# A two-layer decoder trunk on one core: scores and values on parts of the array, first loads by single chunks, bias loads on another queue

## The chip, the cores and the metric

The kernel runs on one core of one Trainium2 chip. The metric is the device time of one execution in microseconds, as the median of several runs. The core has five engines that work side by side and meet at semaphores: TensorE (PE, matmuls; PEld is its load of the stationary operand), VectorE (DVE), ScalarE (ACT), GpSimd (POOL) and SyncE (SP, which here only issues DMAs). Each takes its instructions in the order in which they are written.

## The reference, cut to what matters

The input is 256 tokens of 1024 float32 numbers. Two layers follow, each an attention and a squared-ReLU MLP, with a layer norm behind each:

```python
h = x
for layer in range(2):
    if layer == 0:
        mix = diff_attention(h, ...)       # 8 heads, two maps each, difference of two softmaxes
    else:
        kv = shared_kv(h, w_kv_shared)     # 16 heads of 64
        mix = moba_attention(h, ...)       # here: causal softmax over the one block of 256 keys
    h = layer_norm(ALPHA * h + mix, ...)
    h = layer_norm(ALPHA * h + square(relu(h @ w_up)) @ w_down, ...)
```

All logits get a bias that depends on the distance of query and key (one table for both layers), and the causal mask. In both layers there are 16 maps with a head dimension of 64; the kernel takes them in 8 pairs.

## The kernel before

Weights come as 96 units of 1 MiB, each in two pieces of 128x1024 float32 (`raw`), five of which are in flight or waiting. Each number is split in two: ACT copies the piece to float32r (`whi`, L101), DVE takes the difference (`wlo`, L113). Up to seven split units lie ready. A product is three matmuls that accumulate in PSUM, hi\*hi, hi\*lo, lo\*hi (`three`, L135; lines 139 to 141 and 143 to 145). Every load of a piece is issued on SP's queue (`fetch`, L88) as soon as the piece five earlier has been split; until then that queue stands still, and what is behind it too.

The order on every engine is the order of the program text. `attention` (L334) begins with the V projection. In layer 0 its first two units are taken as they arrive (`v_first`, L377): x comes transposed in four loads of 128x512, each with two loads of 128x512 of a unit. Per step of two chunks, ACT and DVE split x and weights, and TensorE does four hi\*hi matmuls (L395), then the rest (L401, L402). Four matmuls on zeros (L180) run ahead of them. After the first step a product of the bias table with a one-hot matrix, 33 rows by 16 columns (`make_lines`, L187), gives one line per head. DVE copies them out (L188), and ACT's queue copies them 32 times to DRAM, four heads first, twelve later (`copy_lines`, L191), so that tiles with one diagonal per row can be loaded from there (`load_bias`, L198: four loads of 64 KB per pair, on SP's queue, two tiles in turn).

Then a loop over i = 0 to 7 runs a pipeline on pairs: `project(i)` makes Q and K of pair i, transposed, Q's two heads on partitions 0 to 63 and 64 to 127, K's likewise. `halves_hi(i-1)` and `halves_lo(i-1)` split them, `softmax_a(i-2)` adds the bias and takes the exponentials, `softmax_b(i-2)` scales, `turn` and `turned` transpose the maps, `scores(i-1)` and `values(i-3)` end the iteration. For one pair both heads' scores are made at once: the keys lie in `kz`, 128 rows by two halves of 256 columns, where head m's keys fill rows 64m to 64m+63 of half m and zeros fill the rest (memsets on GpSimd, L351). So `halves` needs two ACT copies (L458) and two DVE differences (L468) of 64 rows:

```python
nc.tensor.matmul(s, qh[:, q], kh[:, :, :n], start=True, stop=False)    # L478
nc.tensor.matmul(s, qh[:, q], kl[:, :, :n], start=False, stop=False)   # L479
nc.tensor.matmul(s, ql[:, q], kh[:, :, :n], start=False, stop=True)    # L480
```

once with n = 256 for the later 128 queries (512 columns) and once with n = 128 for the earlier ones (256 columns). Layer 1's values lie in `V` with zeros between the two heads of a pair (L345), and `values` makes both heads' transposed values in one PSUM region with float32 matmuls of 128 stationary columns (L561 to L564). `make_lambda` (L212) loads the four lambda vectors on GpSimd's queue, `rms` runs a reciprocal root on GpSimd (L265 on), `ln_params` (L298) loads the norms' parameters there.

Of the kernel before, what the change touches and what calls it, by code (L numbers as in the profile page):

```python
# [53 lines left out]
def trunk(ctx: ExitStack, tc: tile.TileContext, x, xT, units, lam_a, subln, rel_bias,  # L54
# [13 lines left out]
    def split_to(hi, lo, src, scale=None):  # L68
        """hi + lo = scale * src, both float32r."""
# [13 lines left out]
    def fetch(q):  # L83
        """Piece q's load."""
# [5 lines left out]
    def head():  # L90
        """The hi half of the next piece."""
# [13 lines left out]
    def piece():  # L105
        """The lo half of the next piece, after the hi half of a later one."""
# [12 lines left out]
    def bg(most=8, force=False):  # L119
        """Pieces of later units, as many as the products since the last ones have room for."""  # L120
# [45 lines left out]
    for q in range(4):  # L166
        raws[q] = wpool.tile([P, PIECE], F32, name="raw", bufs=RAWS)
        c = slice(q * 512, (q + 1) * 512)
        nc.sync.dma_start(xTr[:, c], xT[:, c])
        for j in range(2):  # L170
            d = (q % 2) * PIECE + j * 512
            nc.sync.dma_start(raws[q][:, j * 512:(j + 1) * 512], units[q // 2][:, d:d + 512])
# [822 lines left out]
```

## Time and profile before

| | |
|---|---|
| Median of 3 runs | 622.54 us (620.99 to 622.95) |
| Span of the profiled execution, first to last instruction | 621.2 us |
| TensorE busy | 603.8 us, 97% |
| DVE, ACT, GpSimd busy | 385.8, 325.5, 15.4 us |
| DMA | 113.86 MB, mean 183 GB/s |

The profiled execution's time is its span; what lies around it is 1.3 us, if the median of the runs is taken for its time. Starts in the views are microseconds from the span's start. A matmul's duration holds its way through the array, so the pitch from one start to the next says what it costs; weight loads run beside matmuls. A number in brackets at a row's end is the time that the engine sat idle ahead of it, with what ended that.

### The profile page before, as it was taken

Reading aid. Unit: us, or ns where it says so; the run is one execution under the profiler, and the core shown is the slowest. Engines: PE = TensorE matmul, PEld = TensorE weight load, DVE = VectorE, ACT = ScalarE, POOL = GpSimd, SP = SyncE. Lnnn points to the kernel's source line nnn. Section 1 sums busy time; section 2 is a strip of 40 time slices with the busy share of each in tenths; the row PEclk is TensorE's granted clock in tenths of the full one; section 3 lists DMA queues with packets and bytes.
Section 4 is the critical chain, followed back from the end, with each engine's and each line's share of the span. In section 5 each row is a group of like instructions: output and inputs, shape, how many; then the busy total and the mean of one; then the engine's idle time right before and its main releaser. Section 6 shows DMA issues by size and latency. Waiting matters only on the chain.

```text
span 621.2 us, 9556 instructions
## 1 busy us (share of the span) xinstructions
PE 603.8 (97%) x3674; PEld 533.2 (86%) x3674; DVE 385.8 (62%) x706; ACT 325.5 (52%) x556; POOL 15.4 (2%) x40
## 2 busy tenths in 40 slices
PE   8999999999999999999999999999999999999994
PEld 5998987888898899898889899988898898899883
DVE  5479888877634734653877577877767534544236
ACT  5477787447654754552346466462586654554200
POOL 2000011000000000000020000000000000000000
PEclk9999999999999999999999999999999999999998
DMA  8797684547666556556258655341588656553001
GB/s 298 226 312 233 199 257 153 187 169 238 200 222 221 177 197 238 194 178 204 68 165 286 205 157 170 103 143 60 166 303 267 216 179 207 177 181 103 1 0 69
DMA packets 36985, 113.86 MB, mean 183 GB/s; under 512 B 4603, under 2 KB 9756, under 8 KB 36940
## 3 DMA queue, kind: packets, MB, share of 16 engines
q1 hardware_dynamic: 35056, 108.02, 52.9%
q0 software_dynamic: 1264, 4.39, 2.1%
q10 hardware_dynamic: 620, 0.84, 0.4%
q8 instruction: 29, 0.48, 0.3%
q14 instruction: 16, 0.13, 0.1%
HBM read 111.40 MB, written 1.84 MB: 182 GB/s over the span
## 4 chain that ended last, share of the span: by engine, by line
PE 74%; issue 10%; DMA 7%; DVE 5%; ACT 2%; POOL 1%; SPq 0%; DVEq 0%; POOLq 0%; ACTq 0%
PE ps_a L140 11%; PE ps_a L139 11%; PE ps_a L141 11%; PE ps_b L143 9%; PE ps_b L145 9%; PE ps_b L144 9%; DMA raw<-in_units 5%; PE ps_b L141 3%; PE ps_b L139 3%; PE ps_b L140 3%; DVE wlo L113 2%; DMA bias<-scr 1%; ACT whi L101 1%; PE ps_c L288 1%; PE ps_c L533 1%
## 5 line engine op out<-in xcount | busy, mean ns | idle before, releaser
L113 DVE TENSOR_TENSOR wlo<-raw,whi 128x1024 fp32r<-128x1024 f32 x188 | 222.8, 1221 | 66.6 <-ACT whi L101 66.1
L101 ACT ACTIVATE whi<-raw 128x1024 fp32r<-128x1024 f32 x188 | 190.4, 1053 | 83.8 <-PE ps_a L141 49.7
L143 PE MATMUL ps_b<-act_hi,whi 128*128 128x256 f32 x640 | 182.4, 285 | 0.0
L145 PE MATMUL ps_b<-act_hi,wlo 128*128 128x256 f32 x640 | 180.2, 282 | 0.0
L144 PE MATMUL ps_b<-act_lo,whi 128*128 128x256 f32 x640 | 179.9, 281 | 0.0
L144 PEld LDWEIGHTS ps_b<-act_lo,whi 128*128 128x128 f32 x640 | 120.6, 188 | 0.6
L143 PEld LDWEIGHTS ps_b<-act_hi,whi 128*128 128x128 f32 x640 | 120.5, 188 | 0.6
L145 PEld LDWEIGHTS ps_b<-act_hi,wlo 128*128 128x128 f32 x640 | 120.5, 188 | 0.0
L139 PE MATMUL ps_a<-whi,h_hi 128*128 128x512 f32 x248 | 98.5, 397 | 0.0
L141 PE MATMUL ps_a<-whi,h_lo 128*128 128x512 f32 x248 | 98.3, 396 | 0.0
L140 PE MATMUL ps_a<-wlo,h_hi 128*128 128x512 f32 x248 | 98.3, 396 | 0.0
L72 DVE TENSOR_TENSOR h_lo<-sqr,h_hi 128x512 fp32r<-128x512 f32 x24 | 16.6, 692 | 80.5 <-ACT h_hi L70 80.5
L141 PEld LDWEIGHTS ps_a<-whi,h_lo 128*128 128x128 f32 x248 | 46.7, 188 | 11.3
L140 PEld LDWEIGHTS ps_a<-wlo,h_hi 128*128 128x128 f32 x248 | 46.8, 189 | 10.8
L139 PEld LDWEIGHTS ps_a<-whi,h_hi 128*128 128x128 f32 x248 | 46.7, 188 | 10.8
L762 ACT ACTIVATE relu<-ps_b 128x512 f32<-128x512 f32 x32 | 19.1, 596 | 67.1 <-PE ps_b L145 56.8
L500 ACT ACTIVATE t<-t,mx 128x256 f32<-128x256 f32 x64 | 28.4, 444 | 34.5 <-DVE mx L497 34.5
L139 PE MATMUL ps_b<-whi,act_hi 128*128 128x512 f32 x96 | 39.4, 410 | 0.4 <-ACT act_hi L70 0.4
L141 PE MATMUL ps_b<-whi,act_lo 128*128 128x512 f32 x96 | 38.0, 396 | 1.0 <-DVE act_lo L74 1.0
L140 PE MATMUL ps_b<-wlo,act_hi 128*128 128x512 f32 x96 | 37.9, 395 | 0.0
L139 PE MATMUL ps_a<-whi,act_hi 128*128 128x512 f32 x80 | 32.5, 407 | 0.0
L140 PE MATMUL ps_a<-wlo,act_hi 128*128 128x512 f32 x80 | 31.6, 395 | 0.0
(142 smaller groups left out, 628.4 us busy)
## 6 DMA issues: line engine op xcount, KB each, us to landing
raw<-in_units SPq DMA_DIRECT2D x188, 512.0 KB, 5.2
bias<-scr SPq DMA_DIRECT2D x64, 64.0 KB, 4.2
raw<-in_units SPq DMA_DIRECT2D x8, 256.0 KB, 5.3
lnp<-in_ln_g POOLq DMA_DIRECT2D x4, 512.0 KB, 4.3
lnp<-in_ln_b POOLq DMA_DIRECT2D x4, 512.0 KB, 4.9
xres<-in_xT SPq DMA_DIRECT2D x4, 256.0 KB, 5.2
xres<-in_x SPq DMA_DIRECT2D x1, 1024.0 KB
scr<-lnp ACTq DMA_DIRECT2D x1, 576.0 KB
```

Of the source, the lines that this page charges most:

```text
L72: nc.vector.tensor_tensor(lo, src, hi.bitcast(F32), op=ALU.subtract)
L101: nc.scalar.activation(split[v][0][:, c], raws[state["head"]], AF.Copy)
L113: nc.vector.tensor_tensor(split[v][1][:, c], raws.pop(state["piece"]), split[v][0][:, c].bitcast(F32), op=ALU.subtract)
L139: nc.tensor.matmul(ps, a[0], w[0], start=start, stop=False)
L140: nc.tensor.matmul(ps, a[0], w[1], start=False, stop=False)
L141: nc.tensor.matmul(ps, a[1], w[0], start=False, stop=stop)
L143: nc.tensor.matmul(ps, w[0], a[0], start=start, stop=False)
L144: nc.tensor.matmul(ps, w[0], a[1], start=False, stop=False)
L145: nc.tensor.matmul(ps, w[1], a[0], start=False, stop=stop)
L288: nc.tensor.transpose(pt[:, j * P:(j + 1) * P], src[:, j * P:(j + 1) * P], ident)
L500: nc.scalar.activation(t[:, m, s], t[:, m, s], AF.Exp, bias=mx[:, m, j:j + 1], accum_out=sm[:, m, j:j + 1])
L762: nc.scalar.activation(r, ps, AF.Relu)
```

## The change

Four things are changed; everything else is as it was, apart from line numbers and comments.

- The first loads: x comes in eight loads of one chunk (128x256), each with one 128x512 block of a unit. `v_first` works chunk by chunk: split x and weights, two hi\*hi, two lo\*hi, two hi\*lo. Behind the hi\*hi of the first two chunks stands one more matmul on zeros. The bias lines are made after the fifth chunk, copied out of PSUM after both units.
- `copy_lines` and `load_bias` are issued on GpSimd's queue.
- `scores` takes keys without zeros (`kh`, `kl`, 128x256): each head's matmul has the 64 rows in which it lies, the two heads go in turn into two PSUM banks. K is split ahead of Q, in one instruction on ACT and one on DVE.
- In layer 1, `V` has no zeros, and `values` writes each head's 64 PSUM rows with 64 stationary columns.

```diff
-    for q in range(4):
-        raws[q] = wpool.tile([P, PIECE], F32, name="raw", bufs=RAWS)
-        c = slice(q * 512, (q + 1) * 512)
-        nc.sync.dma_start(xTr[:, c], xT[:, c])
-        for j in range(2):
-            d = (q % 2) * PIECE + j * 512
-            nc.sync.dma_start(raws[q][:, j * 512:(j + 1) * 512], units[q // 2][:, d:d + 512])
+    for k in range(NK):
+        if k % 2 == 0:
+            raws[k // 2] = wpool.tile([P, PIECE], F32, name="raw", bufs=RAWS)
+        nc.sync.dma_start(xTr[:, k * S:(k + 1) * S], xT[:, k * S:(k + 1) * S])
+        nc.sync.dma_start(raws[k // 2][:, (k % 2) * 512:(k % 2 + 1) * 512],
+                          units[k // 4][:, (k % 4) * 512:(k % 4 + 1) * 512])
...
     def make_lines():
         nc.tensor.matmul(pb[:NH, :RELS], table, oh[:NBUCKET + 1], start=True, stop=True)
-        nc.vector.tensor_copy(line, pb[:NH, :RELS])
...
-        nc.scalar.dma_start(scr[:, h0:h1].rearrange("p h r -> h p r"),
+        nc.gpsimd.dma_start(scr[:, h0:h1].rearrange("p h r -> h p r"),
...
-            nc.sync.dma_start(b[g:g + COPIES],
+            nc.gpsimd.dma_start(b[g:g + COPIES],
...
+                    a = [at(kk, h) for h in range(2)]
+                    for h in range(2):
+                        nc.tensor.matmul(pv[0, h], a[h][0], hi[:, k], start=kk == 0, stop=False)
+                    if kk < 2:
+                        nc.tensor.matmul(warm[:, :P], zero[:, :P], zero[:, :P], start=True, stop=True)
+                    for h in range(2):
+                        nc.tensor.matmul(pv[0, h], a[h][1], hi[:, k], start=False, stop=False)
+                    for h in range(2):
+                        nc.tensor.matmul(pv[0, h], a[h][0], lo[:, k], start=False, stop=kk == NK - 1)
+                    if kk == 4:
                         make_lines()
...
                 v_first(0)
+                v_first(1)
+                nc.vector.tensor_copy(line, pb[:NH, :RELS])
                 copy_lines(0, 4)
-                v_first(1)
...
+                k = (pool.tile([P, S], F32R, name="kh"), pool.tile([P, S], F32R, name="kl"))
+                nc.scalar.activation(k[0], ps[:, 1], AF.Copy)
                 nc.scalar.activation(q[0], ps[:, 0], AF.Copy, scale=0.125)
-                for m in range(2):
-                    r = slice(m * 64, (m + 1) * 64)
-                    nc.scalar.activation(kz[p % 2][0][r, m], ps[r, 1], AF.Copy)
...
+                sc = [bank("a") for _ in range(2)]
+                for c, n, t in ((0, 256, 1), (256, 128, 0)):
                     q = tokens(t)
-                    nc.tensor.matmul(s, qh[:, q], kh[:, :, :n], start=True, stop=False)
-                    nc.tensor.matmul(s, qh[:, q], kl[:, :, :n], start=False, stop=False)
-                    nc.tensor.matmul(s, ql[:, q], kh[:, :, :n], start=False, stop=True)
+                    for i, (a, b) in enumerate(((qh, kh), (qh, kl), (ql, kh))):
+                        for m in range(2):
+                            r = slice(m * 64, (m + 1) * 64)
+                            nc.tensor.matmul(sc[m][:, c:c + n], a[r, q], b[r, :n], start=i == 0, stop=i == 2)
...
-                v = [slice((3 * p + m) * 64, (3 * p + m + 2) * 64) for m in range(2)]
-                nc.tensor.matmul(o, V[:, 0, v[0]], a[:, 0, 0:256], start=True, stop=False)
-                nc.tensor.matmul(o[:, 128:], V[:, 1, v[0]], a[:, 0, 256:384], start=False, stop=False)
-                nc.tensor.matmul(o[:, 128:], V[:, 1, v[1]], a[:, 1, 256:384], start=False, stop=False)
-                nc.tensor.matmul(o, V[:, 0, v[1]], a[:, 1, 0:256], start=False, stop=True)
+
+                r = [slice(m * 64, (m + 1) * 64) for m in range(2)]
+                v = [slice((2 * p + m) * 64, (2 * p + m + 1) * 64) for m in range(2)]
+                for m in range(2):
+                    nc.tensor.matmul(o[r[m]], V[:, 0, v[m]], a[:, m, 0:256], start=True, stop=False)
+                for m in range(2):
+                    nc.tensor.matmul(o[r[m], 128:], V[:, 1, v[m]], a[:, m, 256:384], start=False, stop=True)
```

On TensorE, in layer 1, the scores of one pair and the values of another stand side by side. Before (shapes are rows of the result by columns; `kz` has a tile's number behind it):

```order
L145 MATMUL ps_b<-act_hi,wlo 128x256
L478 MATMUL ps_a<-kz_3156,qh 128x512 [waits PE_49,Activation_49]
L479 MATMUL ps_a<-kz_3157,qh 128x512 [waits DVE_49]
L480 MATMUL ps_a<-kz_3156,ql 128x512
L478 MATMUL ps_a<-kz_3156,qh 128x256 [waits PE_49]
L479 MATMUL ps_a<-kz_3157,qh 128x256
L480 MATMUL ps_a<-kz_3156,ql 128x256
L561 MATMUL ps_a<-aT,V 128x256 [waits Activation_49]
L562 MATMUL ps_a<-aT,V 128x128
L563 MATMUL ps_a<-aT,V 128x128 [waits DVE_49]
L564 MATMUL ps_a<-aT,V 128x256
L143 MATMUL ps_b<-act_hi,whi 128x256
```

The same place now:

```order
L145 MATMUL ps_b<-act_hi,wlo 128x256
L455 MATMUL ps_a<-kh,qh 128x256 [waits Activation_49]
L455 MATMUL ps_a<-kh,qh 128x256
L455 MATMUL ps_a<-kl,qh 128x256 [waits DVE_49]
L455 MATMUL ps_a<-kl,qh 128x256
L455 MATMUL ps_a<-kh,ql 128x256 [waits DVE_49]
L455 MATMUL ps_a<-kh,ql 128x256
L455 MATMUL ps_a<-kh,qh 128x128 x2
L455 MATMUL ps_a<-kl,qh 128x128 x2
L455 MATMUL ps_a<-kh,ql 128x128 x2
L539 MATMUL ps_a<-aT,V 64x256 [waits Activation_49]
L539 MATMUL ps_a<-aT,V 64x256 [waits DVE_49]
```

Six matmuls of the scores have become twelve of half the columns, and the values' second matmul waits for DVE where the third did. On GpSimd, from its first DMA on, before:

```order
L175 DMA ident<-in_ident 128x128
L351 MEMSET kz_116 128x512
L351 MEMSET kz_117 128x512
L351 MEMSET kz_120 128x512
L351 MEMSET kz_121 128x512
L213 DMA lnp<-in_lam_a 128x256
L215 DMA gsub<-in_subln 128x1
L298 DMA lnp<-in_ln_g 128x1024 [waits DMAHW0_49,DMAHW2_49,DMASW1_49,DMAHW4_49,DVE_49,PE_49]
```

Now (`scr` are the lines' copies in DRAM):

```order
L174 DMA ident<-in_ident 128x128
L189 DMA scr<-lnp 4x32x384 [waits DVE_49]
L196 DMA bias<-scr 32x2x256 [waits DMASW1_49]
L196 DMA bias<-scr 32x2x256 x3
L189 DMA scr<-lnp 12x32x384 [waits DMASW4_49,DMASW5_49,DMASW3_49,DMASW2_49]
L209 DMA lnp<-in_lam_a 128x256
L211 DMA gsub<-in_subln 128x1 [waits DMASW0_49]
L196 DMA bias<-scr 32x2x256 [waits DMASW6_49]
L196 DMA bias<-scr 32x2x256 x3
```

The memsets are gone; lambda's load, which followed them with no wait, stands behind both copies of the lines and the first pair's four bias loads.

## Rows read from the trace of the kernel before

**Rows 1.** The page's head and its part 1: busy time, share, instructions.

```profile
span 621.2 us, 9556 instructions
PE 603.8 (97%) x3674; PEld 533.2 (86%) x3674; DVE 385.8 (62%) x706; ACT 325.5 (52%) x556; POOL 15.4 (2%) x40
```

**Rows 2.** Who waited for whom, TensorE alone: us in total, times, longest.

```profile
PE ps_a L479 <- DVE kz L468: 3.5, 3, 1.4
...
PE ps_a L561 <- ACT aT L540: 0.2, 1, 0.2
```

**Rows 3.** Order of time at the start, TensorE: start, duration, instruction.

```profile
5.98 2.46 PE L395 MATMUL ps_a<-whi,act_hi 128*128 128x512 f32 x4 [0.74 <-ACT whi L70]
...
7.82 0.63 PE L395 MATMUL ps_a<-whi,act_hi 128*128 128x512 f32 x1
8.37 0.82 PE L187 MATMUL ps_c<-lnp,table 33*16 33x384 f32 x1
8.99 0.84 PE L187 MATMUL ps_c<-lnp,table 33*16 33x384 f32 x1
9.76 0.79 PE L401 MATMUL ps_a<-whi,act_lo 128*128 128x512 f32 x1
10.36 0.63 PE L402 MATMUL ps_a<-wlo,act_hi 128*128 128x512 f32 x1
10.78 0.63 PE L401 MATMUL ps_a<-whi,act_lo 128*128 128x512 f32 x1
...
12.88 0.39 PE L402 MATMUL ps_a<-wlo,act_hi 128*128 128x512 f32 x1
13.11 0.39 PE L395 MATMUL ps_a<-whi,act_hi 128*128 128x512 f32 x1
...
21.48 0.28 PE L143 MATMUL ps_b<-act_hi,whi 128*128 128x256 f32 x1
```

**Rows 4.** Busy time by stretch; the last three columns: PEclk, DMA share, GB/s.

```profile
5.90:9.70 3.80, 3.70 (x6) 1.13 (x6) 1.38 (x2) 2.53 (x5) 0.00 (x0) 1.00 0.96 338
```

**Rows 5.** Order of time, ACT and DVE, at four waits in both layers.

```profile
26.93 1.09 ACT L358 ACTIVATE V<-ps_a 128x512 f32<-128x512 f32 x2 [3.89 <-DMA bias<-scr]
...
33.42 0.85 DVE L468 TENSOR_TENSOR kz<-ps_b,kz 64x256 fp32r<-64x256 f32 x2
...
47.25 0.42 DVE L491 CUSTOM_DVE_ANT_0 t<-ps_a,bias 128x256 f32<-128x256 f32 x1 [2.33 <-DMA bias<-scr]
...
349.71 0.42 DVE L491 CUSTOM_DVE_ANT_0 t<-ps_a,bias 128x256 f32<-128x256 f32 x1 [5.76 <-DMA bias<-scr]
```

**Rows 6.** Order of time, TensorE, the scores of layer 0's first pair.

```profile
33.19 0.47 PE L478 MATMUL ps_a<-kz,qh 128*128 128x512 f32 x1
34.42 0.47 PE L479 MATMUL ps_a<-kz,qh 128*128 128x512 f32 x1 [0.76 <-DVE kz L468]
34.73 0.39 PE L480 MATMUL ps_a<-kz,ql 128*128 128x512 f32 x1
34.96 0.28 PE L478 MATMUL ps_a<-kz,qh 128*128 128x256 f32 x1
...
35.31 0.28 PE L143 MATMUL ps_b<-act_hi,whi 128*128 128x256 f32 x1
```

**Rows 7.** DMA issues: operation, queue, count, KB each, median us to landing.

```profile
lnp<-in_lam_a POOLq DMA_DIRECT2D x1, 128.0 KB, 5.9
```

**Rows 8.** Order of time, TensorE, six transposes in layer 1.

```profile
374.36 0.82 PE L533 MATMUL ps_c<-ident,t 128*128 128x128 f32 x6
...
375.13 0.28 PE L144 MATMUL ps_b<-act_lo,whi 128*128 128x256 f32 x1
```

**Rows 9.** Order of time, TensorE, one pair's values in layer 1.

```profile
361.39 0.70 PE L561 MATMUL ps_a<-aT,V 128*128 128x256 f32 x2 [0.24 <-ACT aT L540]
361.93 0.39 PE L562 MATMUL ps_a<-aT,V 128*128 128x128 f32 x2
362.15 0.39 PE L563 MATMUL ps_a<-aT,V 128*128 128x128 f32 x2
```

More of the change, by code (lines that the diff above doesn't have):

```diff
@@ L340, in attention @@
                 tc.tile_pool(name=f"attnc{layer}", bufs=1) as one:
-            V = one.tile([P, 2, D if diff else D + D // 2], F32, name="V")
-            if not diff:
-                for h in range(2):
-                    nc.gpsimd.memset(V[:, h].rearrange("p (a b) -> p a b", a=8)[:, :, 64:128], 0.0)
-            kz = []
-            for i in range(2):
-                z = [one.tile([P, 2, S], F32R, name=f"kz{i}{j}") for j in range(2)]
-                for w in z:
-                    nc.gpsimd.memset(w.bitcast(F32), 0.0)
-                kz.append(z)
+            V = one.tile([P, 2, D], F32, name="V")
             pv = {}
             def v_out(c, h):
-                if diff:
-                    nc.scalar.activation(V[:, h, c * 512:(c + 1) * 512], pv[c, h], AF.Copy)
-                    return
-                src = pv[c, h].rearrange("p (a m d) -> p a m d", m=2, d=64)
-                dst = V[:, h].rearrange("p (a m d) -> p a m d", m=3, d=64)
-                for m in range(2):
-                    nc.scalar.activation(dst[:, 4 * c:4 * c + 4, 2 * m], src[:, :, m], AF.Copy)
+                nc.scalar.activation(V[:, h, c * 512:(c + 1) * 512], pv[c, h], AF.Copy)
             def v_unit(u, c, g):
@@ L384, in v_first @@
                 hi, lo = (w.rearrange("p (k c) -> p k c", k=4) for w in split[u])
-                for j in range(2):
-                    q = 2 * u + j
-                    ks = (2 * j, 2 * j + 1)
-                    split_x(q)
-                    for k in ks:
-                        split_to(hi[:, k], lo[:, k], raws[q][:, (k % 2) * 512:(k % 2 + 1) * 512])
-                    del raws[q]
-                    fetch(q + RAWS)
-                    for k in ks:
-                        for h in range(2):
-                            nc.tensor.matmul(pv[0, h], at(4 * u + k, h)[0], hi[:, k], start=u == k == 0, stop=False)
-                    if q == 0:
-                        make_lines()
-                    for k in ks:
-                        for h in range(2):
-                            a = at(4 * u + k, h)
-                            nc.tensor.matmul(pv[0, h], a[1], hi[:, k], start=False, stop=False)
-                            nc.tensor.matmul(pv[0, h], a[0], lo[:, k], start=False, stop=u == 1 and k == 3)
+                for k in range(4):
+                    q, kk = 2 * u + k // 2, 4 * u + k
+                    split_x(kk)
+                    split_to(hi[:, k], lo[:, k], raws[q][:, (k % 2) * 512:(k % 2 + 1) * 512])
+                    if k % 2:
+                        del raws[q]
+                        fetch(q + RAWS)
+                    a = [at(kk, h) for h in range(2)]
[8 more added lines that the diff above has]
+                    if kk == 4:
+                        make_lines()
                 state["piece"] = state["head"] = (u + 1) * PER
@@ L454, in halves_hi @@
                 q = (pool.tile([P, S], F32R, name="qh"), pool.tile([P, S], F32R, name="ql"))
+                k = (pool.tile([P, S], F32R, name="kh"), pool.tile([P, S], F32R, name="kl"))
+                nc.scalar.activation(k[0], ps[:, 1], AF.Copy)
                 nc.scalar.activation(q[0], ps[:, 0], AF.Copy, scale=0.125)
[L456 to L459 removed]
+                Q[p] = (ps, q, k)
@@ L461, in halves_lo @@
             def halves_lo(p):
-                ps, (qh, ql) = Q[p]
+                ps, (qh, ql), (kh, kl) = Q[p]
+                nc.vector.tensor_tensor(kl, ps[:, 1], kh.bitcast(F32), op=ALU.subtract)
                 nc.vector.scalar_tensor_tensor(ql, ps[:, 0], 0.125, qh.bitcast(F32),
                                                op0=ALU.mult, op1=ALU.subtract)
-                kh, kl = kz[p % 2]
-                for m in range(2):
-                    r = slice(m * 64, (m + 1) * 64)
-                    nc.vector.tensor_tensor(kl[r, m], ps[r, 1], kh[r, m].bitcast(F32), op=ALU.subtract)
```

28 lines of the change are left out of this document (10 added, 18 removed).

## The prediction

> **What bounds the kernel now.** I read the page first: TensorE is busy 603.8 of 621.2 us [rows 1], and its matmuls keep an even pitch, 0.23 us for 512 columns and 0.12 for 256, nearly everywhere. A busy PE row is not proof, since ends are modelled, so the second view is who waited for whom, PE alone: all its waits behind the start come to a few us, and the largest by far is the score matmul L479 on the keys' rest (kz, DVE, L468), 3.5 us in three places; the values wait twice for aT, 0.2 each (the first of two such rows stands there) [rows 2]. So a microsecond more or less on TensorE is one in the end, in every stage; work taken off ACT, DVE or GpSimd counts only where it ends one of those waits. Third view: the order of time at those places and at the start.
>
> **The start** (x and units by single chunks). TensorE begins at 5.98, as soon as ACT has split the first weights; the first projection starts at 21.48 [rows 3]. Between lie 48 matmuls of 512 columns, 11.1 us at the 0.23 that they take from 12.88 on. Up to there they take 0.42, the pitch of the lower of the clock's two levels, although the granted clock reads 1.00 [rows 4]; the pitch changed after matmuls had run without a gap from 9.76 [rows 3]. After the change the first x piece is half as large, so I estimate that weights land some 0.4 us earlier, and each chunk brings six matmuls (2.5 us at the lower level) instead of four that leave a gap; with two small fillers the run without a gap begins near 5.5. If the clock rises as much earlier as the run does, the 11.1 us, the bias product (about 1 us) and the cold part end near 19.6. If it rises at 12.9 as now, nothing is gained. Bounds 0 to -2.2 us; I take -1.8, as the run is what changes. Four more DMA issues on SP's queue have TensorE's backlog as cover: from 13 us on it waits for no load.
>
> **The waits.** Each has one root. At 26.93 ACT has stood 3.89 us, since the second copy of the bias lines sits in its queue and waits for the first bias loads; its halves of Q and K are late, and DVE does the keys' rest last, at 33.42 in two instructions [rows 5]. TensorE waits from 33.19 to 34.42, 1.0 us over the pitch [rows 6]. At 47.25 and 349.71 DVE has stood 2.33 and 5.76 us for a bias tile, whose load stood in SP's queue behind weight loads that wait for buffers [rows 5]; the other two score waits follow within a microsecond. The change puts these DMAs on GpSimd's queue, where a load waits only for its own tile, and does the keys' rest first, in one instruction instead of two. Priced: 3.5 + 0.4 us idle, and for each of five waits 0.24 us of emptied pipeline (33.19 to 34.42 is 1.23, less 0.23 pitch, less the 0.76 noted idle) plus 0.08 to start again (34.42 to 34.73 against 34.73 to 34.96) [rows 6]: 5.5 us. What comes late next: lambda's load. It was issued on GpSimd at once; now it stands behind a copy, four bias loads and the second copy, which waits for these to land. Line ready near 16, three landings in a row at 5 to 6 us (lambda's own took 5.9 [rows 7]) and seven issues between them: lambda lands at about 35, when DVE, no longer held up, could want it at 32 to 35; the keys' rest of the second pair is queued behind it on DVE, needed near 38. I charge 0.5 (bounds 0 to 1.5). Gain 5.0, bounds 3 to 5.8.
>
> GpSimd's own rms step (L265 on) now stands behind the last bias loads, but it waits for ACT far longer. The memsets of kz and V that go away ran on an idle engine; one ACT and one DVE instruction less per pair are off TensorE's path. Nothing for these.
>
> **Scores by halves of the rows.** Before: three matmuls of 512 and three of 256 columns per pair, with zeros in half of the rows: 3 x 0.23 + 3 x 0.12 = 1.05 us [rows 6]. After: twelve of 256 or 128 columns, alternating between upper and lower rows. If the two halves run side by side, the six pairs cost 3 x 0.12, and 3 x 0.11 for the 128-column ones, which are bounded by their weight load: six transposes of 128 columns take 0.65 us, 0.11 each [rows 8]; together 0.69. But the array then changes its shape before and after. The one place that shows it is the bias product L187, 33 rows on a 64-row shape, at the lower clock: it begins 0.55 after its predecessor where the pitch is 0.42, its second pass is followed after 0.77 where the first took 0.62, and the next matmul takes 0.60 instead of 0.42 [rows 3]. So 0.13 to 0.15 to empty the array, and a restart, 0.08 at the upper clock [rows 6]. Half of 0.14 is the lower bound, should it scale with the clock; I take the row as it stands: 0.22 per change of shape, 0.44 per pair. 0.69 + 0.44 = 1.13 against 1.05: +0.08, times 16 pairs +1.2 us. Bounds: -5.9 (no cost of the change) to +11.9 (no concurrency, below).
>
> The Trainium skill, "TensorEngine Tiling (Array Packing)", section Tiling Modes, speaks against this change here: switching the tiling mode drains TensorE. The L187 rows agree; without that rule the time would be the third rival's below, with it the forecast's.
>
> **Second layer's values by halves of the columns.** Before, per pair, two float32 matmuls of 256 and two of 128 columns, two passes each: 0.54 less 0.1 for a restart, and 0.22 for the 128 [rows 9], so 2 x 0.43 + 2 x 0.22 = 1.30. After, side by side: 0.65, plus two changes of shape 0.44: -0.21, times 8 pairs -1.7. In five of eight places values follow scores directly, and one change is shared: 5 x 0.22 = 1.1. Sum -2.8 us; bounds -5.2 to +2.4. The second matmul now needs DVE's half of aT at once, where 0.65 us of other matmuls stood ahead of it; in the loop that copy is issued an iteration's half ahead, so I cost it at nothing; where the cover is gone it costs what the waits for aT cost now, 0.2 us each [rows 2].
>
> **Sum.** -1.8 - 5.0 + 1.2 - 2.8 = -8.4 on the span of 621.2: 612.8. The median of the runs, 622.54, is 1.3 above this span, so **614.1 us**.
>
> **Rivals.**
> First, the halves run one after the other (slower). No row of this kernel shows two small matmuls side by side; TensorE's matmuls start strictly in turn in every window. Then a pair's scores cost 6 x 0.12 + 6 x 0.11 + 0.44 = 1.80, +0.75 x 16 = +11.9, and values 1.30 + 0.44, +0.44 x 8 - 1.1 = +2.4. With start and waits (-6.8): 628.7 + 1.3 = **630.0**. It decides as soon as less than about half of each pair overlaps. Chance 0.16.
> Second, matmuls overlap, weight loads don't: 12 x 0.11 + 0.44 = 1.76 per pair, +11.3; values -2.8: **624.2**, on the edge of slower. For it speaks that each small matmul brings a load of 128 columns, and 0.11 is all that a load ever took [rows 8]; against it that halves lie on different partitions. Chance 0.12.
> Third, the change of shape is nearly free at the upper clock: 43 changes (32 for scores, 16 for values, 5 shared) times 0.22 is 9.5 us: **604.6**. For it: the L187 rows are at the lower clock and one case. Chance 0.16.
> Fourth, the waits stay, in other clothes: lambda or a bias tile is late on GpSimd's queue, where each load is issued by an engine that also waits for landings: 614.1 + 5 = **619.1**. Chance 0.08.
>
> Against the first rival stands the Trainium skill, "TensorE: Matmul & The Clock Gate", Part 3: four row tiles of 512 columns ran there at 3.07 times the speed of one after the other. No row of this kernel shows that.
>
> **How the numbers follow.** The forecast, 614.1, has 0.48; the rivals 0.16, 0.12, 0.16, 0.08. 0.3%, 1.9 us, is about what a measurement of this kernel can tell from no change. Faster than 620.7: forecast, third, fourth mostly, 0.71. Within: the second's lower half and parts of the rest, 0.10. Slower: the first and the second's upper half, 0.19. The range takes in the third rival and the second, and leaves most of the first out: 604 to 627.
>
> **What would show it.** In the trace of after: first projection near 19.6 instead of 21.48; no score matmul that waits for kl over 0.2 us, no DVE wait for bias; DVE's wait for lambda under 1.5 us near 35. In a score group, the two matmuls of a pair start within a few hundredths of each other, and from the last matmul ahead to the first behind it lie 1.1 to 1.2 us; 0.7 to 0.8 means the third rival, 1.8 the first or second (starts 0.11 apart each). The forecast is wrong if the small matmuls keep the pitch of whole ones.

## The result and the profile after

The changed kernel takes 627.27 us (median of 4 runs, 625.82 to 628.13), the kernel before took 621.76 in the same comparison: a ratio of 1.0091, 95% interval 1.0062 to 1.0121. It is slower; 614.1 and faster were forecast, and the time lies just above the range. Yet the page's head and its first part, which answer to [rows 1], show less work on every engine but GpSimd:

```profile
span 626.1 us, 9745 instructions
PE 599.5 (96%) x3774; PEld 527.3 (84%) x3774; DVE 379.5 (61%) x694; ACT 319.2 (51%) x540; POOL 46.3 (7%) x96
```

TensorE is busy 4.3 us less and the span is 4.9 us longer, so TensorE must stand idle or run slowly somewhere. Who waited for whom, TensorE and then DVE, answers to [rows 2]; the third number is the longest single wait:

```profile
PE ps_a L455 <- ACT qh L436: 10.8, 2, 10.2
```

```profile
DVE lp L213 <- DMA lnp<-in_lam_a: 12.9, 1, 12.9
```

The waits for kz are gone, as foreseen. In their place stands one wait of 10.2 us for ACT's half of Q, and DVE stood 12.9 us for lambda's load. TensorE in order of time at that place:

```profile
38.52 0.28 PE L145 MATMUL ps_b<-act_hi,wlo 128*128 128x256 f32 x1
48.97 0.58 PE L455 MATMUL ps_a<-kh,qh 64*128 64x256 f32 x2 [10.17 <-ACT qh L436]
50.58 0.58 PE L455 MATMUL ps_a<-kl,qh 64*128 64x256 f32 x2 [1.02 <-DVE kl L441]
```

From 38.52 to 48.97 nothing starts. Why ACT was late is read from its own waits: it stood 12.6 us at L216, the exponential of lambda's sums, for DVE, which stood for the load. GpSimd's queue in order of time has the root:

```profile
17.80 0.76 POOL L189 DMA_DIRECT2D scr<-lnp  x1 [15.87 <-DVE lnp L388]
27.60 2.13 POOL L196 DMA_DIRECT2D bias<-scr  x4 [9.05 <-DMA scr<-lnp]
37.03 0.69 POOL L189 DMA_DIRECT2D scr<-lnp  x1 [7.29 <-DMA bias<-scr]
37.71 0.60 POOL L209 DMA_DIRECT2D lnp<-in_lam_a  x1
...
47.48 2.15 POOL L196 DMA_DIRECT2D bias<-scr  x4 [8.62 <-DMA scr<-lnp]
```

It is a chain. The first copy of the lines waits for DVE's copy out of PSUM; the first pair's bias tile waits for that copy to land; the second copy waits until these loads have landed, since it writes to the same table `scr`; lambda's load stands behind it; the second pair's tile waits for the second copy. The DMA issues, with KB each and the median time to landing, answer to [rows 7]:

```profile
scr<-lnp POOLq DMA_DIRECT2D x1, 576.0 KB, 10.2
scr<-lnp POOLq DMA_DIRECT2D x1, 192.0 KB, 9.5
lnp<-in_lam_a POOLq DMA_DIRECT2D x1, 128.0 KB, 9.8
gsub<-in_subln POOLq DMA_DIRECT2D x1, 0.5 KB, 9.4
```

Lambda's load took 5.9 us before and 9.8 now. The last view of the place is busy time by stretch (busy time and instructions of each engine, then PEclk, DMA share, GB/s):

```profile
38.40:48.90 10.50, 0.40 (x4) 0.19 (x2) 1.04 (x5) 0.73 (x3) 1.88 (x4) 0.71 0.62 95
48.90:57.00 8.10, 7.00 (x37) 6.55 (x38) 7.82 (x29) 5.25 (x14) 2.83 (x6) 0.53 0.57 164
57.00:64.00 7.00, 7.00 (x65) 6.79 (x64) 6.71 (x21) 5.79 (x18) 3.24 (x7) 1.00 0.80 262
```

TensorE stood, and in the 8.1 us behind the standstill its granted clock was 0.53, about the lower level (1.2 of 2.4 GHz): 37 matmuls where the next 7.0 us hold 65.

**A ledger by stretch** says what this cost and what the rest brought. The bounds are starts of the first score matmul of a layer and of its last group of values, read from TensorE's order of time. The third column is an experiment (one copy, lambda first) that comes below. Each column is one execution, and the sums are of unrounded values.

| us | before | after | one copy, lambda first |
|---|---|---|---|
| to the first score matmul | 33.2 | 31.5 | 31.8 |
| scores to values, layer 0 | 62.2 | 73.6 | 59.3 |
| to the first score matmul of layer 1 | 248.4 | 248.5 | 248.4 |
| scores to values, layer 1 | 69.2 | 64.2 | 64.2 |
| to the end of the last matmul | 199.0 | 199.5 | 201.4 |
| sum | 612.0 | 617.3 | 605.0 |

The changed kernel loses 11.4 us in layer 0's pairs and gains 1.7 and 5.0 elsewhere.

**The array in halves.** One pair of layer 1, scores and values in a row, answers to [rows 6] and [rows 9]:

```profile
367.47 0.28 PE L145 MATMUL ps_b<-act_hi,wlo 128*128 128x256 f32 x1
367.68 0.38 PE L455 MATMUL ps_a<-kh,qh 64*128 64x256 f32 x2
367.90 0.28 PE L455 MATMUL ps_a<-kl,qh 64*128 64x256 f32 x2
368.02 0.28 PE L455 MATMUL ps_a<-kh,ql 64*128 64x256 f32 x2
368.14 0.23 PE L455 MATMUL ps_a<-kh,qh 64*128 64x128 f32 x2
368.20 0.27 PE L455 MATMUL ps_a<-kl,qh 64*128 64x128 f32 x2
368.31 0.27 PE L455 MATMUL ps_a<-kh,ql 64*128 64x128 f32 x2
368.52 0.65 PE L539 MATMUL ps_a<-aT,V 128*64 128x256 f32 x4
369.00 0.39 PE L541 MATMUL ps_a<-aT,V 128*64 128x128 f32 x4
369.32 0.39 PE L143 MATMUL ps_b<-act_hi,whi 128*128 128x256 f32 x1
```

Each line "x2" is the two heads' matmuls, which start within 0.01 us of each other. Pairs of 256 columns follow each other after 0.12 us, the pitch of one whole matmul of 256 columns: the halves run side by side, weight loads too, since pairs of 128 columns follow after 0.06 and 0.11. A change of shape shows twice: the first matmul behind it starts 0.21 after its predecessor instead of 0.12 (the array empties, 0.09), and the one after that 0.22 instead of 0.12 (the restart, 0.10). That is 0.19 per change, at the upper clock, where 0.22 was taken.

**The start.** TensorE's first matmul of values and its first projection answer to [rows 3]:

```profile
6.25 0.74 PE L372 MATMUL ps_a<-whi,act_hi 128*128 128x512 f32 x2 [1.02 <-ACT whi L70]
...
18.92 0.28 PE L143 MATMUL ps_b<-act_hi,whi 128*128 128x256 f32 x1
19.04 0.28 PE L144 MATMUL ps_b<-act_lo,whi 128*128 128x256 f32 x1
19.41 0.39 PE L145 MATMUL ps_b<-act_hi,wlo 128*128 128x256 f32 x1
```

The first projection comes 2.56 us earlier than in [rows 3], and then waits 0.25 for `wlo`: the work has caught up with the loads.

### The profile page after: what moved, and what is told of

It reads as the page before. It is cut to its first block, busy times and chain, and to the rows that moved or that the text cites. A ratio compares the mean times of both kernels' runs of the same rounds, so it can differ in the third digit from the quotient of the medians.

```text
span 626.1 us, 9745 instructions
## 1 busy us (share of the span) xinstructions
PE 599.5 (96%) x3774; PEld 527.3 (84%) x3774; DVE 379.5 (61%) x694; ACT 319.2 (51%) x540; POOL 46.3 (7%) x96
## 4 chain that ended last, share of the span: by engine, by line
PE 85%; DMA 7%; DVE 3%; ACT 2%; issue 1%; SPq 0%; POOL 0%; DVEq 0%; ACTq 0%; POOLq 0%
PE ps_a L141 12%; PE ps_a L140 12%; PE ps_a L139 12%; PE ps_b L143 12%; PE ps_b L145 11%; PE ps_b L144 11%; PE ps_b L141 3%; PE ps_b L139 3%; PE ps_b L140 3%; DMA raw<-in_units 3%; PE ps_a L455 2%; DMA lnp<-in_lam_a 2%; DMA scr<-lnp 2%; PE ps_c L508 1%; DMA bias<-scr 1%; PE ps_c L284 1%
## 5 line engine op out<-in xcount | busy, mean ns | idle before, releaser
L141 PEld LDWEIGHTS ps_a<-whi,h_lo 128*128 128x128 f32 x248 | 46.8, 189 | 11.3
L196 POOL DMA_DIRECT2D bias<-scr x64 | 33.9, 538 | 94.7 <-DVE mx L472 75.2
## 6 DMA issues: line engine op xcount, KB each, us to landing
scr<-lnp POOLq DMA_DIRECT2D x1, 576.0 KB, 10.2
```

The lines of the kernel that those rows point to most:

```text
L141: nc.tensor.matmul(ps, a[1], w[0], start=False, stop=stop)
L196: nc.gpsimd.dma_start(b[g:g + COPIES], bass.AP(tensor=scr.tensor, offset=scr.offset + 2 * p * RELS + P - 1 - g, ap=[[NH * RELS - 1, COPIES ...
```

## The experiments

The first theory put the whole loss on lambda's load, which stands behind the second copy. Its rivals put it on the second pair's bias tile, which hangs on the same copies, or on the other parts of the change.

**Lambda first.** Lambda's two loads stand right behind the identity's at the head of GpSimd's queue.

```diff
     nc.gpsimd.dma_start(ident, ident_in)
+    nc.gpsimd.dma_start(la, ...)
+    nc.gpsimd.dma_start(gsub, subln.rearrange("o p -> p o"))
...
     def make_lambda():
-        nc.gpsimd.dma_start(la, ...)
-        nc.gpsimd.dma_start(gsub, subln.rearrange("o p -> p o"))
```

> The changed kernel with one edit: lambda's two loads are issued on GpSimd's queue right behind the first load there, ahead of the copies of the bias lines, as in the kernel before. Theory A (the loss is lambda's load, which lands at 47.5 us behind the second copy and holds up DVE for 12.9, ACT behind it and TensorE for 10.2 us, and the slow clock behind that): the stall goes, span about 612, 14 us under the changed kernel, and 1.5% faster than the kernel before. Theory B (the matmuls on parts of the array cost the time): no more than 1 us under the changed kernel. Theory C (GpSimd's queue delivers the bias tiles late as well): TensorE still waits at the second pair's scores near 38 us, now for the bias tile through DVE, and the span stays above 618.

Measured: 626.48 us, ratio to the kernel before 1.0082 (1.0052 to 1.0112): next to nothing is won back. Who waited for whom, DVE:

```profile
DVE t L466 <- DMA bias<-scr: 12.1, 2, 11.1
```

and TensorE:

```profile
PE ps_a L455 <- DVE kl L441: 10.6, 2, 10.4
```

The wait is as long as it was, one pair later: now DVE stands for the second pair's bias tile. Lambda alone was not the cause; whatever hangs on the end of the chain holds DVE.

**The queues alone.** The kernel before, with copies and bias loads on GpSimd's queue.

```diff
-        nc.scalar.dma_start(scr[:, h0:h1]...
+        nc.gpsimd.dma_start(scr[:, h0:h1]...
...
-            nc.sync.dma_start(b[g:g + COPIES], ...
+            nc.gpsimd.dma_start(b[g:g + COPIES], ...
```

> The kernel before with the copies of the bias lines and the bias loads on GpSimd's queue and nothing else. Lambda's load then stands behind both copies as in the changed kernel, but the lines are ready at 10 us instead of 17. Theory A: DVE waits for lambda again, some 6 us less than in the changed kernel, and the time is 0 to 8 us above the kernel before, though three waits for bias tiles are gone. Theory B: no part of the array is used alone here, so the time is 3 to 5 us below the kernel before.

Measured: 621.81 us, ratio 1.0000 (0.9968 to 1.0031). The move of the queue by itself costs nothing here: the first copy is issued at 10.23 instead of 17.80, and lambda's load, although it took 11.0 us to land, holds DVE for 5.8 and TensorE waits only 1.3 and 1.2 near there.

**The queues back.** The changed kernel, with the copies on ACT's queue and the bias loads on SP's, as before.

```diff
-        nc.gpsimd.dma_start(scr[:, h0:h1]...
+        nc.scalar.dma_start(scr[:, h0:h1]...
...
-            nc.gpsimd.dma_start(b[g:g + COPIES], ...
+            nc.sync.dma_start(b[g:g + COPIES], ...
```

> The changed kernel with the copies back on ACT's queue and the bias loads back on SP's, and all else as changed. Theory A: lambda's load stands behind nothing, its wait is gone; the start (-2.5 us) and the parts of the array (-3.5 us) stay, the waits for bias tiles come back: 614 to 618. Theory B: 625 or more, since the matmuls on parts of the array are all here.

Measured: 622.61 us, ratio 1.0014 (0.9983 to 1.0045). So the loss is not GpSimd's alone: with the other queues, ACT stands 7.0 us with the second copy in its queue for the first bias loads, TensorE 4.0 for ACT, and the granted clock is 0.73 from 36 to 44 us, behind that. Nor is the move of the queues free everywhere: it costs nothing in the kernel before, and 4.8 us in the changed kernel (1.0014 to 1.0091), where the lines come later.

**The scores alone.** The kernel before with the scores by halves of the rows (keys without zeros, K split first), and nothing else.

```diff
-                    nc.tensor.matmul(s, qh[:, q], kh[:, :, :n], start=True, stop=False)
-                    nc.tensor.matmul(s, qh[:, q], kl[:, :, :n], start=False, stop=False)
-                    nc.tensor.matmul(s, ql[:, q], kh[:, :, :n], start=False, stop=True)
+                    for i, (a, b) in enumerate(((qh, kh), (qh, kl), (ql, kh))):
+                        for m in range(2):
+                            r = slice(m * 64, (m + 1) * 64)
+                            nc.tensor.matmul(sc[m][:, c:c + n], a[r, q], b[r, :n], start=i == 0, stop=i == 2)
```

> The kernel before with the scores by halves of the rows alone (keys without zeros, split ahead of Q). From the changed kernel's rows a pair's group takes 1.26 us from the last whole matmul's start to the second one behind, against 1.29 before: Theory A: -0.4 us by the matmuls and up to -2 by the keys' rest that is ready earlier, so 620 to 622.5. Theory B: 627 or more.

Measured: 621.09 us, ratio 0.9987 (0.9954 to 1.0021): no difference that can be told. Pairs follow one another every 7.73 us in layer 0 in this kernel and before, wherever nothing waits. For layer 1, the first score row of two pairs in a row, before and then in this kernel:

```profile
377.87 0.39 PE L478 MATMUL ps_a<-kz,qh 128*128 128x512 f32 x1
...
386.56 0.39 PE L478 MATMUL ps_a<-kz,qh 128*128 128x512 f32 x1
```

```profile
379.12 0.39 PE L468 MATMUL ps_a<-kh,qh 64*128 64x256 f32 x2
...
387.85 0.38 PE L468 MATMUL ps_a<-kh,qh 64*128 64x256 f32 x2
```

8.69 and 8.73. What the halves save, the two changes of shape take.

**The values alone.** The kernel before with layer 1's values by halves of the columns.

```diff
-                v = [slice((3 * p + m) * 64, (3 * p + m + 2) * 64) for m in range(2)]
-                nc.tensor.matmul(o, V[:, 0, v[0]], a[:, 0, 0:256], start=True, stop=False)
...
+                r = [slice(m * 64, (m + 1) * 64) for m in range(2)]
+                v = [slice((2 * p + m) * 64, (2 * p + m + 1) * 64) for m in range(2)]
+                for m in range(2):
+                    nc.tensor.matmul(o[r[m]], V[:, 0, v[m]], a[:, m, 0:256], start=True, stop=False)
+                for m in range(2):
+                    nc.tensor.matmul(o[r[m], 128:], V[:, 1, v[m]], a[:, m, 256:384], start=False, stop=True)
```

> The kernel before with the second layer's values by halves of the columns alone. The forecast's term was -2.8 us for eight pairs, and the trace of the changed kernel shows 0.80 us a pair next to the scores and 1.47 instead of 1.77 where they stand alone, which is -2.4 to -3.4: 618 to 619.5 us beside 621.5, ratio 0.995 to 0.996. Rival: the array's halves give nothing in time because the vector and scalar engines set the pitch of a pair in that layer: 621.5 us, ratio 0.999 to 1.001.

Measured: 622.04 us, ratio 1.0005 (0.9974 to 1.0037), not the gain that was expected: the interval leaves 0.995 to 0.996 out. The trace shows the gain at its place, and what may hide it. The first score row of two pairs in a row, as above:

```profile
376.43 0.39 PE L468 MATMUL ps_a<-kz,qh 128*128 128x512 f32 x1
...
384.83 0.39 PE L468 MATMUL ps_a<-kz,qh 128*128 128x512 f32 x1
```

8.40 instead of 8.69: 0.3 us a pair, so the rival, that DVE and ACT set the pitch, is wrong. But at 100 us, in work that this kernel shares with the one before, this execution met a stretch at the lower clock (three of its rows):

```profile
100.19 0.80 PE L141 MATMUL ps_b<-whi,act_lo 128*128 128x512 f32 x1 [1.35 <-DVE act_lo L74]
...
101.63 0.63 PE L141 MATMUL ps_b<-whi,act_lo 128*128 128x512 f32 x1
102.06 0.63 PE L139 MATMUL ps_b<-whi,act_hi 128*128 128x512 f32 x1
```

The pitch is 0.43 there where it was 0.23, until 103.3; in the kernel before, behind a wait of 1.0 at the same place, it was not. Whether that happens in most runs of this kernel is not known, so what this part alone is worth in the time of the whole kernel stays open.

The theory after the first four of these runs (values alone was run later), theory D in what follows, was: what costs the time is a chain of transfers that each wait for the one before, about 10 us a copy, begun 7 us later than in the kernel before. Seven runs test it by its beginning, its links and its tail.

**The start alone.** The kernel before with the start by single chunks, the lines' copy behind both units as the change has it, and the queues of before.

```diff
-                    split_x(q)
-                    for k in ks:
-                        split_to(hi[:, k], lo[:, k], ...)
...
+                    split_x(kk)
+                    split_to(hi[:, k], lo[:, k], ...)
...
                 v_first(0)
-                copy_lines(0, 4)
                 v_first(1)
+                nc.vector.tensor_copy(line, pb[:NH, :RELS])
+                copy_lines(0, 4)
```

> The kernel before with the start by single chunks alone (with the lines' copy behind the second unit of values, as the change has it; copies and bias loads on the queues of before). If the start by chunks is good for 2.5 us whatever else happens: 619 us, ratio 0.996. Theory D (the chain of copies and bias tiles starts 7 us later by this, and both ends of it hold ScalarE, whose queue has the second copy, and VectorE): the first projection starts near 19 instead of 21.5, but TensorE waits 4 us or more between 30 and 50 and runs at the lower clock behind it: 622 to 626 us, ratio 1.001 to 1.007.

Measured: 626.14 us, ratio 1.0077 (1.0052 to 1.0102), as the chain theory has it and a little beyond. The first projection starts at 19.48, two us earlier, and then ACT and TensorE read:

```profile
30.70 1.08 ACT L354 ACTIVATE V<-ps_a 128x512 f32<-128x512 f32 x2 [6.12 <-DMA bias<-scr]
```

```profile
36.58 0.77 PE L475 MATMUL ps_a<-kz,qh 128*128 128x512 f32 x1 [5.11 <-ACT kz L455]
```

The part of the change that was to speed up the start costs 4.8 us by itself, with nothing on GpSimd's queue: it makes the lines 7 us later, and the whole chain with them. The run with the queues back has this start and these queues, and the halves besides: 1.0014 against 1.0077, so scores and values by halves are worth 3.9 us together here, though neither shows a gain alone.

**One copy.** The changed kernel, all sixteen lines copied at once; lambda stays behind the first bias tile.

```diff
-                copy_lines(0, 4)
+                copy_lines(0, NH)
                 load_bias(0, 0)
...
-                copy_lines(4, NH)
```

> The changed kernel with one copy of all sixteen heads' lines in place of two (four heads, then twelve); lambda's loads stay behind the first bias tile. Theory D: what held the vector engine is a chain of transfers that each wait for the one before on the same table of lines in memory (first copy, first bias tile, second copy, second bias tile, 8 to 10 us a link), and one copy takes two links out. The copy lands near 29, the first bias tile near 34, lambda near 38 to 41, the second bias tile near 38. Forecast: 612 to 616 us, TensorE's longest wait before 60 us below 4. Rival E: GpSimd's queue is slow whatever lies ahead on it, and lambda's load lands 9 to 10 us behind the bias tile whatever the copies are: lambda after 42, TensorE waits about 5 and runs at the lower clock behind it, 618 to 622.

Measured: 615.87 us, ratio 0.9917 (0.9888 to 0.9946). GpSimd's queue in order of time, and then two of its landing times:

```profile
18.04 0.67 POOL L189 DMA_DIRECT2D scr<-lnp  x1 [16.10 <-DVE lnp L388]
...
30.20 0.58 POOL L209 DMA_DIRECT2D lnp<-in_lam_a  x1
```

```profile
scr<-lnp POOLq DMA_DIRECT2D x1, 768.0 KB, 9.8
...
lnp<-in_lam_a POOLq DMA_DIRECT2D x1, 128.0 KB, 7.7
```

768 KB land in 9.8 us, where 192 KB took 9.5: the second copy was a link for nothing. Each line is 48 KB in every one of these copies (192 for four lines, 768 for sixteen), and the traces hold 11 packets of 3 or 4.6 KB a line in both, 44 and 176. So more lines side by side cost no time here; what a longer line would cost is not shown. TensorE's longest wait behind the start is 1.7 us, and the gain over the kernel before is 5.2 us.

**One copy, lambda first.** Both edits together.

> The changed kernel with one copy of all lines, and lambda's two loads right behind the identity's at the start of GpSimd's queue. Theory D: nothing but the two bias tiles is behind the copy; no wait over 2 us before 60, 610.5 to 613.5 us. Rival E (the queue is slow by itself): the second bias tile lands 8 to 10 us behind the first, near 44, TensorE waits 3 to 5 for the scores of the second pair, 616 to 620.

Measured: 615.41 us, ratio 0.9910 (0.9879 to 0.9941), the fastest of all, though not to be told from the run above. One wait of 1.2 us is left on TensorE between 25 and 62 us; it ends with ACT, which waits for weights. Above the expected 613.5 by 1.9: the ledger's last stretch is 2.4 us longer than before. At 444.16 us, in the last MLP, TensorE has waited 1.9 us for ACT (0.5 in the kernel before), and the granted clock is 0.63 in the 4.6 us behind that; whether most executions have this is not known.

**The lines early.** The changed kernel with two copies, but the lines made and copied after the second chunk of x.

```diff
-                    if kk == 4:
+                    if kk == 1:
                         make_lines()
+                        nc.vector.tensor_copy(line, pb[:NH, :RELS])
+                        copy_lines(0, 4)
...
-                nc.vector.tensor_copy(line, pb[:NH, :RELS])
-                copy_lines(0, 4)
```

> The changed kernel with two copies and lambda's loads where it has them, but the lines made and copied after the second chunk of x, as early as in the kernel before (line out of PSUM near 10 us, not 17). Theory D: the whole chain moves up by about 7 us, lambda lands near 40.5, the second bias tile near 44: TensorE's wait of 10 us falls to 3 to 5, 616 to 620 us. Rival F (the 7 us of lateness does not count, the second copy's 576 KB among the weights does): the chain still ends after 45, 622 to 627.

Measured: 621.73 us, ratio 1.0026 (1.0003 to 1.0050). The chain begins at 10.87 and lambda's load is issued at 31.73 instead of 37.71: of the 6.9 us at the beginning 6.0 arrive. TensorE's long wait falls from 10.2 to this:

```profile
PE ps_a L455 <- ACT qh L436: 5.0, 1, 5.0
```

The long wait halves, but the clock still falls behind it (0.50 from 43.5 to 50.0), and the time lies between what theory D and rival F allowed: the lateness counts, and does not make up all of the loss.

**All three.** Lines early, one copy, lambda first.

> The changed kernel with the lines made early, one copy of all sixteen heads and lambda's loads at the start of the queue. Theory D: both bias tiles are there before 32, nothing waits for a transfer of GpSimd's queue: 610 to 613 us. Rival G (what was lost near 50 was not the transfers but the clock, which falls whenever the scores of the first pairs start): a stretch at the lower clock of 5 us or more stays near 45 to 57 without a wait ahead of it, 615 or more.

Measured: 617.35 us, ratio 0.9938 (0.9908 to 0.9968), not better than one copy alone. Theory D's time is missed. Nothing waits for GpSimd's queue any more; rival G is not what stands there either, since the lower clock (0.83 from 35 to 45) follows a wait of 2.9 us for ACT. But TensorE's first matmul of values begins at 6.83 and waited 1.6 us for its weights, the pitch of 512 columns is 0.42 up to 11 us, the first projection starts at 22.08, and ACT waits up to 3.4 us for weights behind that. Lambda's early loads alone do not explain it: the version with one copy and lambda first has the same loads there, begins at 5.96 and reaches the first projection at 19.06. The first row of each, all three and then one copy with lambda first:

```profile
6.83 1.22 PE L372 MATMUL ps_a<-whi,act_hi 128*128 128x512 f32 x2 [1.61 <-ACT whi L70]
```

```profile
5.96 0.74 PE L372 MATMUL ps_a<-whi,act_hi 128*128 128x512 f32 x2 [0.76 <-ACT whi L70]
```

With two tables, without these loads, the pitch is 0.42 up to 10 us too. So the start of this execution was a late one; why the median of ten runs misses theory D's time is open.

**One copy in the kernel before**, as a control.

```diff
-                copy_lines(0, 4)
+                copy_lines(0, NH)
...
-                copy_lines(4, NH)
```

> The kernel before with one copy of all sixteen lines in place of two, on the queues that it has. Control: if the second copy is a burden of the kernel before as well (ScalarE waited 3.9 us for the first bias tile ahead of the second copy, VectorE 9.0 us for bias tiles near 47), this gains 2 to 4 us, 617.5 to 619.5, and that much of what one copy gave the changed kernel is no part of the change. Theory D without a burden in the kernel before (its chain starts 7 us earlier and just fits): 620.5 to 622.5, ratio within 0.002 of 1.

Measured: 622.77 us, ratio 1.0026 (0.9999 to 1.0053). The kernel before gains nothing by one copy, so what it brings the changed kernel undoes a loss that came with the change. (The 9.0 us of the expectation are DVE's waits for bias tiles in the whole execution; near 47 us they are 2.3.)

**Two tables.** The changed kernel, its two copies and their order as they are, but the first four heads' lines in a table of their own, so that the second copy does not wait for the first bias loads.

```diff
-    scr = dram.tile([COPIES, NH, RELS], F32, name="scr")
+    scr_a = dram.tile([COPIES, 4, RELS], F32, name="scr_a")
+    scr_b = dram.tile([COPIES, NH - 4, RELS], F32, name="scr_b")
...
+        scr, h, n = (scr_a, 2 * p, 4) if p < 2 else (scr_b, 2 * p - 4, NH - 4)
```

> The changed kernel with its two copies, its order on GpSimd's queue and its bytes as they are, but the table of lines in two pieces of memory: the first four heads' and the other twelve's. So the second copy no longer waits until the first bias tile has been read, and the second pair's bias tile (heads two and three) no longer waits for the second copy. Theory D (the links are what counts, not the copies' bytes or the queue): the second copy starts near 30 instead of 37, lambda lands near 38 to 41 instead of 47.5, the second bias tile before 38: 614 to 618 us, ratio 0.988 to 0.995. Rival H (the 576 KB of the second copy hold up what is queued behind them, whatever they wait for): lambda and the second bias tile land 10 us or more behind the second copy's issue, TensorE's wait is 5 to 10: 619 to 624 us.

Measured: 621.40 us, ratio 0.9990 (0.9966 to 1.0014), within what rival H allowed, and not what theory D did. GpSimd's queue, then lambda's landing:

```profile
29.70 0.71 POOL L190 DMA_DIRECT2D scr_b<-lnp  x1
30.39 0.62 POOL L211 DMA_DIRECT2D lnp<-in_lam_a  x1
```

```profile
lnp<-in_lam_a POOLq DMA_DIRECT2D x1, 128.0 KB, 11.2
```

The link is gone: the second copy starts at 29.70 instead of 37.03, and the ratio falls from 1.0091 to 0.9990. But lambda's load still lands only when the copy ahead of it does, at 41.6, and TensorE waits 3.8 and 1.4 us and runs at 0.59 of its clock from 43.0 to 50.5. So the loss has two roots: links that wait for each other (1.0091 to 0.9990, 6.3 us), and a small load queued behind a large copy on one queue (0.9990 to 0.9917 with one copy, 4.5 us). One copy takes away both. That the 4.5 us are lambda's is read from the trace, where DVE waits 7.1 us for lambda and for no bias tile; no run has two tables and lambda first.

## Why the prediction was wrong

**What bounds the kernel.** Right: TensorE's order is the time, and each gain and loss above is one on TensorE.

**The waits: the step that failed.** "Line ready near 16, three landings in a row at 5 to 6 us ... lambda lands at about 35 ... I charge 0.5 (bounds 0 to 1.5)." The line was ready near 17, and the chain was the one described; the landings were not. The first copy took 9.8 us (17.80 to 27.60), the bias loads 7.3 behind the last issue, lambda's load 9.8, and it came at 47.5 instead of 35. The price came from lambda's own load with no copy ahead of it [rows 7], and the trace of before had a nearer row, which I did not price. There the first copy is issued on ACT, and the loads that wait for it on SP:

```profile
10.45 0.28 ACTq L191 DMA_DIRECT2D scr<-lnp  x1
```

```profile
21.79 1.75 SPq L198 DMA_DIRECT2D bias<-scr  x4
```

11.3 us from the copy's issue to the first load behind it. By that row, with the line ready at 17, the first bias loads go out at 28 to 30, land near 36 by the 5 to 6 us that I gave them, and the second copy's 11.3 put the second pair's loads at 47, where they came (47.48). As that tile is wanted near 38, the upper bound of the charge would have been 9 us instead of 1.5. And a standstill has a second price, the clock: of 14.3 us that layer 0's pairs lose against the version with one copy, 10.2 lie in the distance of the first two pairs' scores (17.5 against 7.3 us), and 4.1 in the next (11.2 against 7.1), of which TensorE stood only 1.0 idle.

**The fourth rival had the mechanism,** "the waits stay, in other clothes: lambda or a bias tile is late on GpSimd's queue", with a chance of 0.08 and a price of 5 us. Read from the ledger, the price is 14.3: it ends at 619.1 + 9.3 = 628.4 instead of 619.1, beside 627.27. That it comes so near is partly luck: by the medians the price is 11.2 (1.0091 against 0.9910), and the gains beside it were smaller than forecast too (below). It was a case on the other side, and I had it on the near one, because its price came from the same row of 5.9 us.

**What comes late next.** The prediction followed lambda's load through the chain, but not the chain's beginning: the start by chunks makes the lines later, and I counted that only as "line ready near 16". The start alone, with the queues of before, costs 4.8 us; the queues alone cost nothing; the chain's lateness and its links make the loss together.

**The other terms,** seen in the ledger and in the version with one copy:

- *The start, -1.8.* First projection 2.56 us earlier, first score 1.7 earlier. Right in these two traces, which show why it is more at first and less later: the pitch was near 0.23 from 6.25 on, so the clock was at the upper level earlier than I gave it, and then TensorE waits for weights. But this level is not the start's alone. With the old start the first projection comes at 21.48 to 22.18 in four traces and at 19.12 in the fifth (one copy in the kernel before), where the pitch is 0.23 from 9 us on; with the new one it comes at 18.72 to 19.83 in seven traces, and at 20.81 and 22.08 in the two with a pitch of 0.42 up to 10 or 11 us (two tables, all three). So the gain is a tendency over executions, and part of it in this pair can be chance.
- *The waits, -5.0.* Read from single traces: in layer 1 the scores of the third pair follow those of the second after 7.42 us instead of 9.09, -1.7, and those of the fourth after 8.18 instead of 9.52, -1.3, of which 0.5 is the pair's own gain; in layer 0 the version with one copy and lambda first has -2.9. That is -5.4, less 0.6 for a new wait for DVE's `t` at the end of layer 1's pairs: as priced, once the chain is short. The third pair's distance is as short with either cause alone taken away, 7.40 with the queues alone and 7.42 with the scores alone, so for that pair the two parts do not add up.
- *Scores by halves, +1.2.* The halves do run side by side, the first two rivals fall, and a change of shape costs 0.19, not 0.22; the third rival falls too. 7.73 us a pair in layer 0 with and without: 0.0 in place of +0.08 each.
- *Layer 1's values, -2.8.* -0.30 a pair alone (8.40 against 8.69), -0.50 with scores next to them (8.18 to 8.19 against 8.69), where the shared change of shape counts: 5 x 0.50 + 3 x 0.30 = -3.4 by an estimate from these distances. The mechanism was right and the size 0.6 short at its place; the run with this part alone does not show it in the whole time.

The rule that a change of shape costs time stands: the Trainium skill, "TensorEngine Tiling (Array Packing)", section Tiling Modes, says that a switch drains TensorE, and the trace has 0.09 us for the emptying at the upper clock, 0.19 with the restart.

With the chain shortened the direction would have been right, and not the whole size: 0.9917 and 0.9910 are 5.2 and 5.6 us under the kernel before, where -8.4, a ratio of 0.986, was forecast; both intervals leave that out. In the ledger, one execution each, the last column is 7.0 us under the first. That the clock's fall belongs to the loss rests on stretches at the lower level behind the long waits (0.53, 0.50 and 0.59 behind idle stretches of 10.5, 5.0 and 3.8 us); no run kept the wait and took the lower clock away.

## What to carry to other kernels

Before moving a step, follow every transfer that hangs on it to its last reader, and price each link by the nearest row of its own kind (from issue to the issue of what waits for it), not by a transfer that stood alone on its queue. Two copies into one table with a read between them are a chain of three links; where a copy of more lines lands no later, as here, one copy is shorter. Put small loads that somebody waits for ahead of the copies, not behind them; and add to an idle stretch of several us on TensorE what the lower clock costs behind it.

## What was not expected of the hardware

- A copy of lines to memory lands after 9.5, 10.2 and 9.8 us for 192, 576 and 768 KB, which are 4, 12 and 16 lines of 48 KB: the number of lines does not count in this range. No run changed the size of a line.
- A load of 0.5 KB took 9.4 us behind lambda's load and the copy of 576 KB on GpSimd's queue, 7.5 us behind lambda's load and four bias loads (one copy).
- Halves of the array's rows run side by side down to the weight loads: pairs of 256 columns every 0.12 us, the pitch of one whole matmul, and pairs of 128 columns every 0.06 to 0.11.
- Short idle stretches of like length were followed by either level of the clock: 1.2 us by none lower (one copy, lambda first), 1.4 us by 3 us at a pitch of 0.43 instead of 0.23 (values alone), 1.7 us by a clock of 0.79 in the 8.2 us behind (one copy). That may be part of the scatter of the runs; no run here tests it.
